# A low part of the weights on GpSimd once a block, and eight blocks a layer by seven products

## The chip, the cores and the metric

The kernel runs on one core of a Trainium2 chip. The metric is the device time of one execution in microseconds (us), as the median of several executions. Five engines work side by side, each through its own queue: TensorE (PE, with its weight loads as PEld), VectorE (DVE), ScalarE (ACT), GpSimd (POOL) and SyncE (SP).

## The reference

One decoder layer on 256 tokens of width 2048, all in float32: a gated feed-forward part, a token mixer, and a second feed-forward part, each with a residual and a layer norm. The change touches the two feed-forward parts alone.

```python
def swiglu(h, w_in, w_out):                       # w_in 2048 x 11264, w_out 5632 x 2048
    a, b = jnp.split(h @ w_in, 2, axis=-1)
    return (jax.nn.silu(a) * b) @ w_out

h = layer_norm(DN_ALPHA * h + 0.5 * swiglu(h, ffn1_w_in[l], ffn1_w_out[l]), ln1_g[l], ln1_b[l])
...                                               # attention, recurrent branch, merge, ln2
h = layer_norm(DN_ALPHA * h + 0.5 * swiglu(h, ffn2_w_in[l], ffn2_w_out[l]), ln3_g[l], ln3_b[l])
```

## The kernel before

**High and low parts.** TensorE multiplies in a rounded float format, so every operand is held as a high part (rounded) and a low part (the rest), and each product is three matmuls: high by high, high by low, low by high (`three`, lines 623 to 625). The activations are stationary and the weights stream. The weights come from HBM as float32 and are split on the way by `Weights.split_to`: ScalarE writes the high part `wh` (L217), VectorE subtracts it from the source and writes the low part `wl` (L218).

**Pieces.** The weights are one long list of pieces, in the order in which TensorE uses them. A plain piece is 128x1024 (two k-tiles by 512 columns); it is loaded into one of four `raw` buffers. The split runs four pieces ahead of TensorE (`AHEAD`), the load eight; `wh` and `wl` have five buffers each. `Weights.unit` hands TensorE the next slice and, at the start of each piece, sends off loads and splits.

**Blocks.** The input product of a feed-forward part is cut into 22 blocks of 512 columns (256 of each half). `blockF` runs one block over 16 k-tiles, as four chunks of four k-tiles. A chunk is done in one of two ways:

- plain (two pieces "c"): 4 k-tiles x 2 token tiles x 3 = 24 matmuls of 512 columns;
- by seven products in place of eight (Strassen's scheme; pieces `p1q3`, `p2`, `q5p7`, `q4p6` from one 128x2048 chunk `rf`, two buffers): 42 matmuls of 256 columns. Three sums of weight quarters are made on VectorE first (`Weights.operand`: `ws` of 1024 elements at L190, two of 512 at L194 and L197), and 3.5 pieces are split instead of two.

`block_plan` writes the order of a block's pieces. It also places pieces "o" there, the fills: plain pieces of the output product of an earlier segment, three at the start of a block from block 6 on and a fourth in the middle. When a fill has finished an output tile, ScalarE scales it (L960) and GpSimd issues a transfer that adds it to Y (L961). `FOUR` lists the blocks with all four chunks by seven products; from block 6 on, the others have chunk 0 plain. Blocks 0 and 1 are plain, block 2 has chunks 1 and 3 by seven products, blocks 3 to 5 have three. The last pieces of a part (`OUT_LAST`) are all plain.

**The join.** The seven products leave partial results in four PSUM banks. After a block, `gate` (inside `ffn`) joins them in the SBUF tile `z`, four quarters of 256: a copy on ScalarE (L920), then VectorE's joins, each with one input in PSUM (L921, L922, L923, L927 twice), then silu on ScalarE and the product on VectorE (L933). A block whose four chunks all go by seven products has a second L927 of 256 elements instead of 512.

**Who orders what.** The queues of TensorE, SyncE and GpSimd are in the order in which the code issues. Those of VectorE and ScalarE are ordered by a planner; `gate`'s first part is issued with high priority. Each engine runs its queue strictly in order.

Of the kernel before, what the change touches and what calls it, by code (L numbers as in the profile page):

```python
# [8 lines left out]
F32 = mybir.dt.float32  # L9
# [3 lines left out]
OP = mybir.AluOpType  # L13
AX = mybir.AxisListType.X

P = 128
# [5 lines left out]
NBK = NKF // 2  # L22
# [39 lines left out]
FORMS = ("p1q3", "p2", "q5p7", "q4p6")  # L62
# [6 lines left out]
def block_plan(chunks, fills, lead=2, n=4, late=True):  # L69

    plain = [("c", k) for q in range(n) if q not in chunks for k in (4 * q, 4 * q + 2)]
    forms = [(f, q) for q in chunks for f in FORMS]
    rest = ["o"] * fills
    plan = [(rest.pop(), 0) for _ in range(min(lead, fills))] + plain[:1]
    plain = plain[1:]
    slow = []
    while plain or rest:
        for which in (plain, rest) if late else (rest, plain):  # L80
            if which:
                p = which.pop(0)
                slow.append((p, 0) if p == "o" else p)
    if not forms:
        return plan + slow
    step = len(forms) / (len(slow) + 1)
    n = 0
    for i, f in enumerate(forms):
        plan.append(f)
        while len(slow) > n and i + 1 >= (n + 1) * step:  # L90
            plan.append(slow[n])
            n += 1
    return plan


FOUR = (9, 12, 15, 18, 21)


def layer_plans():
    three = (1, 2, 3)  # L100
    plans = [block_plan((), 0)] * 2
    plans += [block_plan((1, 3), 2, 0)] + [block_plan(three, 2, 2, late=False)] * 3
    for n in range(6, NBK):
        plans.append(block_plan(FAST if n in FOUR else three, 4, 3))
    return plans


FILLS = [(g, nb, 2 * p) for g, (b0, b1) in enumerate(SEGS[:-1]) for nb in range(4) for p in range(b1 - b0)]
PLANS = layer_plans()
PLAN_A = block_plan(FAST_A, 0, 0)  # L110
GATE_FAST = ((), (), (), (3,), FAST_A, FAST_A, (), ())
YA_FAST = ((), (0, 1), (0, 1), (0, 1))
# [4 lines left out]
MG_FORMS = (0, 1)  # L117
LAG_MG = (7, 4)
A_ORDER = (6, 7, None, 4, 5, 0, 1, 2, 3)
assert sum(f == "o" for p in PLANS for f, _ in p) == len(FILLS)  # L120

OUT_LAST = ([(nb, k) for nb in (0, 1) for k in (0, 2, 4)] + [(nb, 6) for nb in (0, 1)]
            + [(nb, k) for nb in (2, 3) for k in (0, 2, 4, 6)])
# [1 line left out]
LAG_T = (7, 6)  # L125
# [5 lines left out]
class Weights:  # L131
# [8 lines left out]
    def __init__(self, nc, pool, pieces, on_piece):  # L140
        self.nc, self.pool, self.on_piece = nc, pool, on_piece
        self.fast_pool = None
        self.pieces = pieces
        self.raw = {}
        self.sums = {}
        self.hl = {}
        self.loaded = 0
        self.split = 0
        self.cur = -1
        self.limit = None  # L150
        self.off = 0
# [50 lines left out]
    def split_to(self, i, step=PIECE):  # L202
        nc = self.nc
        while self.split <= min(i, len(self.pieces) - 1):
            form = self.pieces[self.split][1]
            self.load_to(self.split)
            k = self.key(self.split)
            h = self.pool.tile([P, PIECE], F32R, name=f"wh{self.split}", tag="wh", bufs=HL_BUFS)
            l = self.pool.tile([P, PIECE], F32R, name=f"wl{self.split}", tag="wl", bufs=HL_BUFS)
            n = self.size(self.split)  # L210
            if form:
                parts = [(self.operand(k, form), *(x[:, :n].rearrange("p (f r c) -> p f r c", r=2, c=256)
                                                   for x in (h, l)))]
            else:
                parts = [tuple(x[:, q:min(n, q + step)] for x in (self.raw[k], h, l)) for q in range(0, n, step)]
            for src, hp, lp in parts:
                nc.scalar.activation(hp, src, AF.Copy)  # L217
                self.last = nc.vector.tensor_tensor(lp, src, hp, op=OP.subtract)  # L218
            self.hl[self.split] = (h, l)
            if form in (None, FORMS[-1]):  # L220
                del self.raw[k]
            self.split += 1

    def unit(self, n):
        if self.cur < 0 or self.off == self.size(self.cur):
# [61 lines left out]
def tile_layer(ctx, tc, x_fm, x_tm, pos, f1a, f1o, wA, wki, wB, wG, lru, wab, wrb, wo, f2a, f2o,  # L287
               cols_d, ln1_g, ln1_b, ln2_g, ln2_b, ln3_g, ln3_b, out):
    nc = tc.nc
# [41 lines left out]
    def block_pieces(ap, plan, fills=None, fo=None):  # L331
        chunk = {}
        for f, k in plan:
            if f == "c":
                pieces.append((ap[:, k * 512:k * 512 + PIECE], None))
            elif f == "o":
                g, nb, k = next(fills)
                k += 2 * SEGS[g][0]
                pieces.append((fo[nb][:, k * 512:k * 512 + PIECE], None))
            else:  # L340
                if k not in chunk:
                    chunk[k] = ap[:, k * 2048:(k + 1) * 2048]
                pieces.append((chunk[k], f))

    def ffn_pieces(fa, fo):
        fills = iter(FILLS)
        for n, plan in enumerate(PLANS):
            block_pieces(fa[n], plan, fills, fo)
        for nb, k in OUT_LAST:
            k += 2 * SEGS[-1][0]  # L350
            plain([fo[nb][:, k * 512:k * 512 + PIECE]])

    ffn_pieces(f1a, f1o)
    for i, b in enumerate(A_ORDER):
        if b is None:
            plain([wki])
# [20 lines left out]
    for nb in range(3):  # L377
        block_pieces(wo[nb], block_plan(MG_FAST[nb], 0, 0))
    plain([wo[3]])
    ffn_pieces(f2a, f2o)  # L380

    W = Weights(nc, pool, pieces, bg.step)
    W.fast_pool = ctx.enter_context(tc.tile_pool(name="f1", bufs=1))
    lane, first_home, shared = [None], {}, ExitStack()

# [523 lines left out]
        if ln.last:  # L909
            ln.finish()  # L910

    def ffn(x, forms, ln):
        def gate(c, e, g, i, lag, plain):

            z = W.fast_pool.tile([P, 4 * S], F32, name=name("z"), tag="z", bufs=Z_BUFS)
            z4 = z.rearrange("p (j c) -> p j c", j=4)
            a, b = z4[:, 0:4:2], z4[:, 1:4:2]
            if e:
                p1, p6, p7, q5 = e[0][:, :S], e[0][:, S:], e[1][:, :S], e[1][:, S:]
                A.activation(z4[:, 0], p1, AF.Copy)  # L920
                V.tensor_tensor(z4[:, 1], z4[:, 0], p6, op=OP.add)  # L921
                V.tensor_tensor(z4[:, 2], z4[:, 1], p7, op=OP.add)  # L922
                V.tensor_tensor(b, q5[:, None, :].to_broadcast([P, 2, S]), z4[:, 1:3], op=OP.subtract)  # L923
                for t in range(2):
                    w = 512 if plain or t == 0 else S
                    zt = z[:, t * 512:t * 512 + w]
                    V.tensor_tensor(zt, zt, c[t][:, :w], op=OP.add)  # L927
                A.activation(a, a, AF.Silu)
            else:
                for t in range(2):  # L930
                    A.activation(z4[:, 2 * t], c[t][:, :S], AF.Silu)
                    A.activation(z4[:, 2 * t + 1], c[t][:, S:], AF.Copy)
            V.tensor_tensor(a, a, b, op=OP.mult)  # L933
            for _ in range(lag):
                yield
            ps = BP()
            for k in range(2):
                for t in range(2):
                    T.transpose(ps[:, k * S + t * P:k * S + (t + 1) * P], z[:, t * 512 + k * P:t * 512 + (k + 1) * P], ident)  # L939
            for k in range(2):  # L940
                hl = UHL("g")
                split(hl, ps[:, k * S:(k + 1) * S])
                g[i + k] = hl

        g = [[None] * (2 * (b1 - b0)) for b0, b1 in SEGS]
        fills = iter(FILLS)
        open_ps = []

        def fill():
            s, nb, k0 = next(fills)  # L950
            if k0 == 0:
                open_ps[:] = MM(), MM()
            for k in (k0, k0 + 1):
                w = W.unit(512)
                for t in range(2):
                    tokens(open_ps[t], g[s][k], t, w, k == 0, k == len(g[s]) - 1)
            if k0 + 2 == len(g[s]):
                for t in range(2):
                    u = W.fast_pool.tile([P, 512], F32, name=name("yd"), tag="yd", bufs=2)
                    A.activation(u, open_ps[t], AF.Copy, scale=0.5)  # L960
                    G.dma_start(Y[t][nb], u, accum_op=OP.add)  # L961

        for s, (b0, b1) in enumerate(SEGS):
            for n in range(b0, b1):
                c, e = blockF(x, forms, PLANS[n], fill)
                task = gate(c, e, g[s], 2 * (n - b0), LAG_T[n == NBK - 1], ("c", 0) in PLANS[n])
                with tc.high_priority():
                    next(task)
                bg.add("gate", task)
        new_stats()  # L970
        if not ln.last:
            share("t")
            bg.add("main", later(consts(), W.last.ins))
        out_product(g[-1], ln, pair=True)
# [7 lines left out]
                G.dma_start(away[t][nb], Y[t][nb])  # L982

    ln = InnerNorm("ln1_g", "ln1_b", FAST_A, put_away)
    ffn(xs, xf, ln)
    hs = ln.hs


# [346 lines left out]
    share("s")  # L1335


    ffn(ln.hs, ln.forms, OuterNorm(ln3_g, ln3_b))


def _layout(x, positions, ffn1_w_in, ffn1_w_out, ln1_g, ln1_b, w_in, conv_w, conv_b, lru_wa, lru_ba,
# [73 lines left out]
```

## Time and profile before

| | |
|---|---|
| median of 3 runs | 2387.85 us (2387.63 to 2387.97) |
| profiled execution | 2390.11 us, span 2388.3 us |
| TensorE busy | 2364.0 us, 99% |
| VectorE busy | 2213.3 us, 93% |
| ScalarE busy | 1502.0 us, 63% |
| GpSimd busy | 123.1 us, 5% |
| granted TensorE clock | 0.998 |

The span is the time from the first to the last instruction that the profiler saw; the execution's own time is a little longer. Matmul durations overlap in the records, so work on TensorE is read from starts. In the rows of the profile, L218 is line 218 of the kernel before, `out<-in` are the tiles, and what follows `<-` is what ended an idle time.

### The profile page before, as it was taken

The page shows a single profiled execution, that of the slowest core. Times are in us where ns is not written, and L with a number is a line of the kernel's source. Part 1 is how long each engine was busy: PE and PEld are TensorE (multiplying, and loading weights), DVE is VectorE, ACT ScalarE, POOL GpSimd, SP SyncE. Part 2 cuts the span into 40 slices and gives each one's busy share as a digit, 9 for nine tenths or more (in the row PEclk, how much of TensorE's full clock was granted, in tenths as well). Part 3 has the DMA queues.
Part 4 walks back from the last instruction along what each step waited for, and adds up shares of the span by engine and source line. Part 5 has one row for each costly group of instructions (what it writes and reads, how often), then busy time and mean ns, then how long its engine had stood idle before and what let it go on. Part 6 is the DMA issues. An engine that isn't in the chain of part 4 may idle for free.

```text
span 2388.3 us, 38774 instructions
## 1 busy us (share of the span) xinstructions
PE 2364.0 (99%) x14890; PEld 2111.6 (88%) x14890; DVE 2213.3 (93%) x3127; ACT 1502.0 (63%) x2042; POOL 123.1 (5%) x196
## 2 busy tenths in 40 slices
PE   8999999999999999999999999999999999999997
PEld 6898999989988888888999998888898899899996
DVE  7999999999999998789788888998999999999997
ACT  7666666666647554665588885555766666666662
POOL 0000000000000000001000001100000000000000
PEclk9999999999999999999999999999999999999999
DMA  8666666666666455547655568755675666666665
GB/s 293 193 222 213 227 212 217 219 217 212 195 210 221 177 186 179 187 142 265 207 183 185 187 191 295 252 194 175 209 229 212 221 212 188 230 227 212 216 208 176
DMA packets 123018, 501.24 MB, mean 210 GB/s; under 512 B 14256, under 2 KB 14256, under 8 KB 101968
## 3 DMA queue, kind: packets, MB, share of 16 engines
q1 hardware_dynamic: 104256, 454.60, 54.6%
q0 software_dynamic: 18576, 44.17, 8.1%
q8 instruction: 116, 1.90, 0.3%
q14 instruction: 70, 0.57, 0.1%
HBM read 467.26 MB, written 10.49 MB: 200 GB/s over the span
## 4 chain that ended last, share of the span: by engine, by line
PE 92%; DVE 5%; issue 1%; DMA 1%; ACT 0%; SPq 0%; POOL 0%; DVEq 0%; ACTq 0%; POOLq 0%
PE mm L625 20%; PE mm L623 20%; PE mm L624 20%; PE bp L624 6%; PE bp L623 6%; PE bp L625 6%; PE mm L1248 4%; PE mm L1249 4%; PE mm L1247 4%; DVE wl L218 2%; PE bp L939 1%; DVE ws L190 0%; ACT wh L217 0%; DMA raw<-f1a 0%; PE bp L1128 0%
## 5 line engine op out<-in xcount | busy, mean ns | idle before, releaser
L217 ACT ACTIVATE wh<-raw 128x1024 fp32r<-128x1024 f32 (+2 forms) x540 | 552.3, 1044 | 293.3 <-PE mm L625 169.0
L218 DVE TENSOR_TENSOR wl<-raw,wh 128x1024 fp32r<-128x1024 f32 (+2 forms) x540 | 637.2, 1196 | 96.4 <-ACT wh L217 94.7
L217 ACT ACTIVATE wh<-rf 128x1024 fp32r<-128x1024 f32 (+1 forms) x489 | 439.9, 915 | 313.6 <-PE mm L625 157.3
L218 DVE TENSOR_TENSOR wl<-rf,wh 128x1024 fp32r<-128x1024 f32 (+1 forms) x489 | 505.5, 1040 | 12.8 <-ACT wh L217 7.1
L623 PE MATMUL mm<-wh,hs 128*128 128x512 f32 (+1 forms) x884 | 317.0, 359 | 0.0
L625 PE MATMUL mm<-wh,hs 128*128 128x512 f32 (+1 forms) x884 | 311.1, 352 | 1.1 <-DVE hs L804 1.1
L624 PE MATMUL mm<-wl,hs 128*128 128x512 f32 (+1 forms) x884 | 310.8, 352 | 0.2 <-DVE wl L218 0.2
L625 PE MATMUL mm<-wh,g 128*128 128x512 f32 x704 | 278.2, 395 | 0.2 <-DVE g L747 0.2
L623 PE MATMUL mm<-wh,g 128*128 128x512 f32 x704 | 278.2, 395 | 0.0
L624 PE MATMUL mm<-wl,g 128*128 128x512 f32 x704 | 278.1, 395 | 0.0
L217 ACT ACTIVATE wh<-ws 128x1024 fp32r<-128x1024 f32 x163 | 173.0, 1061 | 141.9 <-PE mm L625 83.9
L623 PE MATMUL bp<-wh,sh 128*128 128x256 f32 x918 | 258.7, 282 | 0.0
L624 PE MATMUL bp<-wl,sh 128*128 128x256 f32 x918 | 256.4, 279 | 1.2 <-DVE wl L218 1.2
L625 PE MATMUL bp<-wh,sl 128*128 128x256 f32 x918 | 256.2, 279 | 0.0
L190 DVE TENSOR_TENSOR ws<-rf 128x1024 f32<-128x1024 f32 x163 | 198.4, 1217 | 7.0 <-DMA rf<-f1a 1.4
L218 DVE TENSOR_TENSOR wl<-ws,wh 128x1024 fp32r<-128x1024 f32 x163 | 198.2, 1216 | 2.8 <-ACT wh L217 2.4
L625 PEld LDWEIGHTS mm<-wh,hs 128*128 128x128 f32 x884 | 165.9, 188 | 27.5 <-DVE hs L804 2.5
L623 PEld LDWEIGHTS mm<-wh,hs 128*128 128x128 f32 x884 | 166.1, 188 | 24.3 <-issue 1.3
L624 PEld LDWEIGHTS mm<-wl,hs 128*128 128x128 f32 x884 | 166.1, 188 | 22.4 <-DVE wl L218 0.7
L1249 PE MATMUL mm<-hs,wl 128*128 128x256 f32 x640 | 179.8, 281 | 0.0
L1247 PE MATMUL mm<-hs,wh 128*128 128x256 f32 x640 | 179.8, 281 | 0.0
L1248 PE MATMUL mm<-hs,wh 128*128 128x256 f32 x640 | 179.8, 281 | 0.0
(312 smaller groups left out, 5291.8 us busy)
## 6 DMA issues: line engine op xcount, KB each, us to landing
rf<-f1a SPq DMA_DIRECT2D x64, 1024.0 KB, 5.4
rf<-f2a SPq DMA_DIRECT2D x64, 1024.0 KB, 5.6
raw<-f1o SPq DMA_DIRECT2D x88, 512.0 KB, 6.5
raw<-f2o SPq DMA_DIRECT2D x88, 512.0 KB, 6.6
raw<-wB SPq DMA_DIRECT2D x80, 512.0 KB, 4.1
raw<-wG SPq DMA_DIRECT2D x54, 512.0 KB, 4.3
raw<-f2a SPq DMA_DIRECT2D x48, 512.0 KB, 4.8
raw<-f1a SPq DMA_DIRECT2D x47, 512.0 KB, 5.3
```

What stands on the lines that cost most here:

```text
L190: v.tensor_tensor(t, b[:, 0:4:3], b[:, 1:2].to_broadcast([P, 2, 2, 256]), op=OP.add)
L217: nc.scalar.activation(hp, src, AF.Copy)
L218: self.last = nc.vector.tensor_tensor(lp, src, hp, op=OP.subtract)
L623: T.matmul(ps, xh, w[0], start=start, stop=False)
L624: T.matmul(ps, xh, w[1], start=False, stop=False)
L625: T.matmul(ps, xl, w[0], start=False, stop=stop)
L939: T.transpose(ps[:, k * S + t * P:k * S + (t + 1) * P], z[:, t * 512 + k * P:t * 512 + (k + 1) * P], ident)
L1247: T.matmul(ps[:, :S], w[0], x[:, 0], start=first, stop=False)
L1248: T.matmul(ps[:, :S], w[0], x[:, 1], start=False, stop=False)
L1249: T.matmul(ps[:, :S], w[1], x[:, 0], start=False, stop=last)
```

## The change

Three things. First, `FOUR` has eight blocks, every second one from 7 to 21, instead of five, and the first layer's block 2 has three chunks by seven products instead of two (`EARLY`, with a plan for each layer). Second, for each block that has a chunk by seven products, one plain piece two or three places into the next block is noted in `late`; `split_to` lets ScalarE make its high part as before, but puts the low part aside. Third, `gate` calls `late_parts` after the first join: GpSimd copies one element that this join wrote into a small tile, and then makes the low part that was put aside. That is 20 copies and 20 subtractions in each of the two feed-forward parts. The condition for the wide last join is now read from the plan's plain pieces in general.

```diff
-FOUR = (9, 12, 15, 18, 21)
-
-
-def layer_plans():
+FOUR = (7, 9, 11, 13, 15, 17, 19, 21)
+EARLY = (((), (), (1, 2, 3)), ((), (), (1, 3)))
+
+
+def layer_plans(early):
     three = (1, 2, 3)
-    plans = [block_plan((), 0)] * 2
-    plans += [block_plan((1, 3), 2, 0)] + [block_plan(three, 2, 2, late=False)] * 3
+    plans = [block_plan(early[n], 0) for n in range(2)]
+    plans += [block_plan(early[2], 2, 0)] + [block_plan(three, 2, 2, late=False)] * 3
     for n in range(6, NBK):
         plans.append(block_plan(FAST if n in FOUR else three, 4, 3))
     return plans
...
-PLANS = layer_plans()
+PLANS = [layer_plans(e) for e in EARLY]
...
                 nc.scalar.activation(hp, src, AF.Copy)
-                self.last = nc.vector.tensor_tensor(lp, src, hp, op=OP.subtract)
+                if self.split in self.late:
+                    self.waiting.append((lp, src, hp))
+                else:
+                    self.last = nc.vector.tensor_tensor(lp, src, hp, op=OP.subtract)
...
+    def late_parts(self, mark):
+
+        for lp, src, hp in self.waiting:
+            t = self.pool.tile([P, 32], F32, name=f"go{self.split}", tag="sm", bufs=20)
+            self.nc.gpsimd.tensor_copy(t[:, :1], mark)
+            self.nc.gpsimd.tensor_tensor(lp, src, hp, op=OP.subtract)
+        self.waiting = []
...
-    def ffn_pieces(fa, fo):
+    def ffn_pieces(fa, fo, plans):
         fills = iter(FILLS)
-        for n, plan in enumerate(PLANS):
+        ends = []
+        for n, plan in enumerate(plans):
             block_pieces(fa[n], plan, fills, fo)
+            if any(f in FORMS for f, _ in plan):
+                ends.append(len(pieces))
         for nb, k in OUT_LAST:
             k += 2 * SEGS[-1][0]
             plain([fo[nb][:, k * 512:k * 512 + PIECE]])
+        late.extend([i for i in (e + 3, e + 2) if not pieces[i][1]][0] for e in ends if not all(pieces[i][1] for i in (e + 2, e + 3)))
...
                 A.activation(z4[:, 0], p1, AF.Copy)
                 V.tensor_tensor(z4[:, 1], z4[:, 0], p6, op=OP.add)
+                W.late_parts(z4[:, 1, :1])
                 V.tensor_tensor(z4[:, 2], z4[:, 1], p7, op=OP.add)
                 V.tensor_tensor(b, q5[:, None, :].to_broadcast([P, 2, S]), z4[:, 1:3], op=OP.subtract)
...
-                task = gate(c, e, g[s], 2 * (n - b0), LAG_T[n == NBK - 1], ("c", 0) in PLANS[n])
+                task = gate(c, e, g[s], 2 * (n - b0), LAG_T[n == NBK - 1], any(f == "c" for f, _ in plans[n]))
```

More of the change, by code (lines that the diff above doesn't have):

```diff
@@ L119 @@
 A_ORDER = (6, 7, None, 4, 5, 0, 1, 2, 3)
-assert sum(f == "o" for p in PLANS for f, _ in p) == len(FILLS)
+assert sum(f == "o" for p in PLANS[0] for f, _ in p) == len(FILLS)
 OUT_LAST = ([(nb, k) for nb in (0, 1) for k in (0, 2, 4)] + [(nb, 6) for nb in (0, 1)]
@@ L142, in __init__ @@
         self.fast_pool = None
+        self.late = set()
+        self.waiting = []
         self.pieces = pieces
@@ L222, in split_to @@
             self.split += 1
+    def late_parts(self, mark):
[3 more added lines that the diff above has]
+            self.nc.gpsimd.tensor_tensor(lp, src, hp, op=OP.subtract)
+        self.waiting = []
     def unit(self, n):
@@ L351, in ffn_pieces @@
             plain([fo[nb][:, k * 512:k * 512 + PIECE]])
-    ffn_pieces(f1a, f1o)
+        late.extend([i for i in (e + 3, e + 2) if not pieces[i][1]][0] for e in ends if not all(pieces[i][1] for i in (e + 2, e + 3)))
+    late = []
+    ffn_pieces(f1a, f1o, PLANS[0])
     for i, b in enumerate(A_ORDER):
@@ L379, in tile_layer @@
     plain([wo[3]])
-    ffn_pieces(f2a, f2o)
+    ffn_pieces(f2a, f2o, PLANS[1])
     W = Weights(nc, pool, pieces, bg.step)
+    W.late.update(late)
     W.fast_pool = ctx.enter_context(tc.tile_pool(name="f1", bufs=1))
@@ L910, in out_product, with ffn @@
             ln.finish()
-    def ffn(x, forms, ln):
+    def ffn(x, forms, ln, plans):
         def gate(c, e, g, i, lag, plain):
@@ L964, in ffn @@
             for n in range(b0, b1):
-                c, e = blockF(x, forms, PLANS[n], fill)
-                task = gate(c, e, g[s], 2 * (n - b0), LAG_T[n == NBK - 1], ("c", 0) in PLANS[n])
+                c, e = blockF(x, forms, plans[n], fill)
+                task = gate(c, e, g[s], 2 * (n - b0), LAG_T[n == NBK - 1], any(f == "c" for f, _ in plans[n]))
                 with tc.high_priority():
@@ L984, in tile_layer @@
     ln = InnerNorm("ln1_g", "ln1_b", FAST_A, put_away)
-    ffn(xs, xf, ln)
+    ffn(xs, xf, ln, PLANS[0])
     hs = ln.hs
@@ L1335, in tile_layer @@
     share("s")
-    ffn(ln.hs, ln.forms, OuterNorm(ln3_g, ln3_b))
+    ffn(ln.hs, ln.forms, OuterNorm(ln3_g, ln3_b), PLANS[1])
 def _layout(x, positions, ffn1_w_in, ffn1_w_out, ln1_g, ln1_b, w_in, conv_w, conv_b, lru_wa, lru_ba,
```

## The prediction

> **What bounds the kernel now.** I read the page first: shares, the chain that ended last, and what TensorE waits for.
>
> ```profile
> span 2388.3 us, 38774 instructions
> ...
> PE 2364.0 (99%) x14890; PEld 2111.6 (88%) x14890; DVE 2213.3 (93%) x3127; ACT 1502.0 (63%) x2042; POOL 123.1 (5%) x196
> ...
> PE 92%; DVE 5%; issue 1%; DMA 1%; ACT 0%; SPq 0%; POOL 0%; DVEq 0%; ACTq 0%; POOLq 0%
> ...
> L624 PE MATMUL mm<-wl,hs 128*128 128x512 f32 (+1 forms) x884 | 310.8, 352 | 0.2 <-DVE wl L218 0.2
> ...
> L624 PE MATMUL bp<-wl,sh 128*128 128x256 f32 x918 | 256.4, 279 | 1.2 <-DVE wl L218 1.2
> ```
>
> TensorE is busy 99% of the span and 92% of the last chain. VectorE follows closely at 93%, yet TensorE's waits for the low parts that VectorE makes (L218) are only 1.2 + 0.2 = 1.4 us in all. So TensorE's count of columns sets the time, and VectorE just keeps up. How closely, I read from the busy time in three consecutive blocks in mid-layer, cut at the first join (L921) of each block: block 12 (all four chunks by seven products, "F"), then 13 and 14 (three chunks so and one plain, "T").
>
> ```profile
> core 0: us, PE busy (x) PEld busy (x) DVE busy (x) ACT busy (x) POOL busy (x), PEclk, DMA share, GB/s
> 355.13:386.40 31.27, 31.27 (x222) 29.07 (x221) 31.05 (x39) 20.92 (x26) 1.75 (x2) 1.00 0.70 213
> 386.40:418.10 31.70, 31.70 (x203) 28.46 (x202) 30.72 (x38) 20.29 (x25) 1.75 (x2) 1.00 0.65 221
> 418.10:450.29 32.19, 32.19 (x205) 28.84 (x204) 31.63 (x39) 19.71 (x25) 1.75 (x2) 1.00 0.62 214
> ```
>
> TensorE is busy for the whole of each at full granted clock (1.00). The three last 31.27 + 31.70 + 32.19 = 95.16 us, VectorE is busy for 31.05 + 30.72 + 31.63 = 93.40, so it is idle for 1.76 us in three blocks, 0.59 us a block. Any VectorE work beyond that becomes TensorE's wait.
>
> **TensorE's gain.** Durations of matmuls overlap, so I take starts, in the timeline of TensorE.
>
> ```profile
> 384.73 0.40 PE L623 MATMUL mm<-wh,g 128*128 128x512 f32 x1
> ...
> 387.52 0.40 PE L623 MATMUL mm<-wh,g 128*128 128x512 f32 x1
> ...
> 390.56 0.39 PE L624 MATMUL mm<-wl,g 128*128 128x512 f32 x1
> ...
> 395.93 0.28 PE L623 MATMUL bp<-wh,xs 128*128 128x256 f32 x1
> ...
> 445.81 0.28 PE L623 MATMUL bp<-wh,sh 128*128 128x256 f32 x1
> ...
> 448.61 0.40 PE L623 MATMUL mm<-wh,g 128*128 128x512 f32 x1
> ```
>
> From 387.52 to 395.93 stand three plain pieces, 36 matmuls of 512 columns: 8.41 / 36 = 0.2336 us each. From 445.81 to 448.61 stand 24 of 256 columns: 2.80 / 24 = 0.1167 us. A plain chunk is 24 of the former, 5.61 us; by seven products it is 42 of the latter, 4.90 us. A converted chunk gives 0.70 us. FOUR has eight blocks instead of five in each of two layers, and block 2 of the first layer gets a third chunk: 3 + 3 + 1 = 7 chunks, 7 x 0.705 = 4.9 us.
>
> **VectorE's price.** Starts again, at the end of block 12:
>
> ```profile
> 386.40 0.41 DVE L921 TENSOR_TENSOR z<-z,bp 128x256 f32<-128x256 f32 x1
> 386.73 1.22 DVE L218 TENSOR_TENSOR wl<-raw,wh 128x1024 fp32r<-128x1024 f32 x1
> 387.87 0.41 DVE L922 TENSOR_TENSOR z<-z,bp 128x256 f32<-128x256 f32 x1
> 388.20 1.22 DVE L190 TENSOR_TENSOR ws<-rf 128x1024 f32<-128x1024 f32 x1
> 389.33 0.68 DVE L923 TENSOR_TENSOR z<-bp,z 128x512 f32<-128x512 f32 x1
> 389.93 1.21 DVE L218 TENSOR_TENSOR wl<-rf,wh 128x1024 fp32r<-128x1024 f32 x1
> 391.07 1.01 DVE L927 TENSOR_TENSOR z<-z,mm 128x512 f32<-128x512 f32 x2
> 392.00 0.68 DVE L194 TENSOR_TENSOR rf<-ws,rf 128x512 f32<-128x512 f32 x1
> 392.60 0.68 DVE L218 TENSOR_TENSOR wl<-rf,wh 128x512 fp32r<-128x512 f32 x1
> ```
>
> Start to start, 1024 elements take 1.14 us, 512 take 0.60, a 256-wide join 0.33. A chunk by seven products needs three operand sums (1.14 + 0.60 + 0.60) and four low parts (3 x 1.14 + 0.60): 6.36. The plain chunk needs two low parts, 2.28, and a join that is 512 wide instead of 256, 0.27 more. So F costs VectorE 3.81 us more than T, and TensorE 0.70 less. From the three blocks: T is (93.40 - 3.81) / 3 = 29.86 for VectorE and (95.16 + 0.70) / 3 = 31.95 for TensorE, F is 33.67 and 31.25. With F and T in turn, a pair needs 63.5 us of VectorE and 63.2 of TensorE. Eight F blocks alone would overload VectorE by 0.3 us a pair.
>
> **What GpSimd takes off.** One low part a block, 1.14 us: 2 x 1.14 from a pair, which leaves VectorE 61.26 against 63.20. That is 0.97 us of spare a block, more than today's 0.59. Over the kernel 40 low parts leave VectorE (46 us) and 7 x 3.81 = 27 come. If the spare lasts, all of the 4.9 us arrive; where GpSimd's work costs VectorE over 0.97 us a block, it turns into TensorE's wait.
>
> **The added waits.** GpSimd copies one element of z after the first join, then subtracts. The copy waits for VectorE; behind it in GpSimd's queue are only the two transfers to Y of the next block's fill, due half a block later, and ScalarE's two buffers for those. The join into z's second and fourth quarters must now wait for that copy, since it overwrites what the copy reads, and all of VectorE's queue stands behind it. Rows for two such copies elsewhere in the kernel (VectorE's timeline, then GpSimd's) and, by groups, for GpSimd's DMA issues:
>
> ```profile
> 2356.33 1.21 DVE L218 TENSOR_TENSOR wl<-raw,wh 128x1024 fp32r<-128x1024 f32 x1
> ```
>
> ```profile
> 2356.48 1.10 POOL L856 COPY row<-st 128x1 f32<-128x1 f32 x1 [32.66 <-DVE st L757]
> ...
> 2358.98 0.22 POOL L856 COPY row<-st 128x1 f32<-128x1 f32 x1
> ```
>
> ```profile
> L961 POOL DMA_DIRECT2D y<-yd x80 | 70.1, 982 | 1212.5 <-ACT yd L960 1162.3 <-DVE rf L194 24.9 <-DVE wl L218 24.6
> L1200 POOL DMA_DIRECT2D gf<-gd x24 | 12.9, 540 | 11.1 <-DVE y L606 4.7 <-PE bp L1310 2.3 <-DVE y L608 1.2
> ```
>
> A copy alone takes 0.22 us. The one that started 0.15 us into a VectorE subtraction took 1.10 and ended at 2357.58, 0.04 after the subtraction did (2356.33 + 1.21). So a VectorE operation with both inputs in SBUF holds GpSimd off. In the changed program's instruction order one such operation (ws, 1.14, or rf, 0.60) and the second join stand between the first join and the join that waits; the copy can end while the second join runs, so I put this wait at nothing. If that cover were gone it would be up to 1.1 us a block, just over the spare.
>
> No row shows a 128x1024 subtraction on GpSimd. It is at least VectorE's 1.22 us, as I see no reason for it to be quicker. From above, its deadline bounds it. The late piece after a T block that an F block follows is the third fill: the next block began at 384.73, two pieces of 2.80 later its low part is read at 390.56, and the first join began at 386.40, so 4.16 us are left. After an F block the piece is the fourth, 2.80 later: 6.96 us. I take about 2.4 us, twice VectorE's: ends 3.5 to 4.0 us after the first join, inside both.
> The Trainium skill (GPSIMD Engine Reference, Performance versus the Vector engine) gives 4497 ns for an add of 2048 fp32 elements; half of it, my estimate from that page, is 2.25 us, and the sum stays as it is.
>
> Elsewhere: SyncE's queue is unaffected, since the raw buffer that frees some microseconds later is wanted four plain pieces on, most of a block. ScalarE gets seven times 1.5 pieces more and stands at 63%.
>
> **The sum.** Profiled execution 2390.11 us; less 4.9 for the columns; less 0.4 of the 1.4 us of waits for low parts (each early block gets 1.14 of relief, but the first layer's block 2 gets 3.81 of new work): 2384.8. The median of the runs lies 2.26 below the profiled execution (2387.85): **2382.5 us**.
>
> **Rival 1, slower: VectorE is held off in its turn.** The copy's row shows one direction. If GpSimd's subtraction, once begun, likewise holds off VectorE's operations with two SBUF inputs, only joins (one input in PSUM) can run beside it. In the changed order the joins aren't consecutive: after the first stand a two-input operation, the second join (0.33), a two-input low part, the third join (0.60), and then the last joins at once (T) or after another two-input sum (F). If GpSimd starts before that low part, VectorE loses 2.3 of the 2.4 us each time, 4.6 a pair: 61.26 + 4.6 = 65.9 against 63.4 now (two thirds of 95.16), 2.4 x 16 pairs = 39 us slower. If it starts one operation later, it has 1.80 us of joins beside it in T and 0.60 in F: the loss is 0.6 + 1.8, a pair 63.7, 0.2 x 16 = 4 us slower. It decides from 0.97 us a block. Range 2392 to 2427, middle 2409. For it: that one row. Against it: no VectorE operation in the rows above is drawn out, and the 80 transfers that L961 issues beside it are stretched themselves (0.98 against 0.54).
> The Trainium skill (SBUF — State Buffer, SBUF: two separate sides) speaks against this change: the port pair that both engines share is an exclusive lock for a whole instruction, in either direction. The copy agrees for one direction; by the page the time is this rival's.
>
> **Rival 2: the gain is eaten.** VectorE loses about what it was relieved of, 1 us a block; TensorE waits at the end of F blocks for part of what it gained: 2384 to 2392.
>
> **Rival 3, slower: GpSimd is late.** It waits through two or three VectorE operations and ends 5 us after the first join; the third fill waits 0.8 us at each of 8 x 2 such ends: 13 us, less the 4.9 gained: 2396. The deadline of 4.16 us is close; for F ends nothing happens.
>
> **How the numbers follow.** 0.2%, about what a measurement of this kernel can tell from no change, is 4.8 us: faster is below 2383.1. The forecast, with all of the spare left, has 0.56, between 2381 (all 1.4 us of waits gone too) and 2384.5; 0.45 of it below 2383.1. Rival 2 has 0.12, all within. Rival 1 has 0.24, 0.20 of it slower and 0.04 within; rival 3 has 0.08, slower. That makes 0.45, 0.27 and 0.28. The range goes from 2381 into rival 1, to 2402, beyond which lies some 0.17.
>
> **What would show it.** Right: block 12 and its like still without TensorE gaps, F and T in turn taking 63.2 us a pair, GpSimd's subtraction near 2.4 us, VectorE's spare near 1 us a block, its operations no longer than 1.22 us beside GpSimd. Rival 1: a two-input VectorE operation of 2 to 3.5 us, or a hole of that size, beside each subtraction, and TensorE waiting for L218's successor in F blocks. Rival 3: TensorE waiting for GpSimd at the third fill. A pair over 63.4 us makes the forecast wrong.

## The result: slower by 2.2%

| | before | after |
|---|---|---|
| median | 2387.77 us (2387.63 to 2387.97, 4 runs) | 2440.39 us (2439.81 to 2441.06, 4 runs) |
| profiled execution, span | 2390.11, 2388.3 | 2439.81, 2438.0 |

The ratio is 1.0218, 95% interval 1.0206 to 1.0231: 52.6 us slower. The forecast was 2382.5, the range ended at 2402. The mechanism is the prediction's Rival 1, in its strong case.

The page of the changed kernel: the span, the busy times, the shares of the chain that ended last, and three groups of TensorE's matmuls with their idle time and what ended it.

```profile
span 2438.0 us, 39174 instructions
...
PE 2378.7 (98%) x15016; PEld 2118.5 (87%) x15016; DVE 2279.0 (93%) x3122; ACT 1500.4 (62%) x2056; POOL 248.5 (10%) x276
...
PE 56%; DVE 28%; issue 11%; ACT 4%; DMA 1%; ACTq 0%; DVEq 0%; POOL 0%; SPq 0%; POOLq 0%
...
L643 PE MATMUL mm<-wh,hs 128*128 128x512 f32 (+1 forms) x872 | 312.1, 358 | 5.4 <-DVE z L948 5.4
...
L644 PE MATMUL mm<-wl,g 128*128 128x512 f32 x704 | 280.4, 398 | 15.8 <-DVE wl L224 15.8
...
L644 PE MATMUL bp<-wl,sh 128*128 128x256 f32 x924 | 261.1, 283 | 9.8 <-DVE wl L224 9.8
```

VectorE has five instructions fewer than before and is busy for 66 us more. Its share of the last chain went from 5% to 28%, and TensorE's waits for low parts (L218 before, L224 now) from 1.4 us to 25.8 (15.8 and 9.8 in these rows, 0.2 in a group that isn't shown). TensorE never waits for GpSimd.

The same stretch as in the prediction, cut at the first join (now L941), for an F block's window and a T block's:

```profile
463.04:496.64 33.60, 31.98 (x221) 29.20 (x220) 33.31 (x38) 20.46 (x26) 4.70 (x4) 1.00 0.68 210
496.64:529.10 32.46, 32.28 (x205) 28.62 (x203) 32.28 (x37) 19.70 (x25) 5.24 (x4) 1.00 0.59 205
sum 66.06, PE 64.26 PEld 57.82 DVE 65.60 ACT 40.16 POOL 9.94; mean PE 32.13 PEld 28.91 DVE 32.80 ACT 20.08 POOL 4.97
```

A pair takes 66.06 us; two thirds of the three blocks before were 63.44. The cause is in VectorE's timeline at the end of a T block, beside GpSimd's, and in one row from the end of an F block:

```profile
463.04 0.42 DVE L941 TENSOR_TENSOR z<-z,bp 128x256 f32<-128x256 f32 x1
463.37 0.69 DVE L200 TENSOR_TENSOR rf<-rf 128x512 f32<-128x512 f32 x1
463.97 0.42 DVE L943 TENSOR_TENSOR z<-z,bp 128x256 f32<-128x256 f32 x1
464.30 2.70 DVE L224 TENSOR_TENSOR wl<-rf,wh 128x512 fp32r<-128x512 f32 x1
466.93 0.68 DVE L944 TENSOR_TENSOR z<-bp,z 128x512 f32<-128x512 f32 x1
...
498.44 3.23 DVE L224 TENSOR_TENSOR wl<-rf,wh 128x1024 fp32r<-128x1024 f32 x1
```

```profile
463.52 0.58 POOL L234 COPY go<-z 128x1 f32<-128x1 f32 x1 [4.38 <-DVE z L941]
464.06 2.39 POOL L235 TENSOR_TENSOR wl<-raw,wh 128x1024 fp32r<-128x1024 f32 x1
...
498.20 2.39 POOL L235 TENSOR_TENSOR wl<-raw,wh 128x1024 fp32r<-128x1024 f32 x1
```

GpSimd's subtraction runs from 464.06 to 466.45. The join L943, which has one input in PSUM, ends beside it as always. The next operation has both inputs in SBUF and takes 2.70 us instead of 0.68: it ends at 467.00, 0.55 after GpSimd has let go. At the end of the F block a low part of 1024 takes 3.23 instead of 1.22. This happens at 38 of the 40 subtractions; the last one of each part stands beside other work. So a subtraction holds VectorE for 2.0 us and has taken 1.14 off it: some 77 us of hold over the kernel, against 46 us of relief.

### The profile page after: what moved, and what is told of

It reads as the page before. It is cut to its first block, busy times and chain, and to the rows that moved or that the text cites. A ratio compares the mean times of both kernels' runs of the same rounds, so it can differ in the third digit from the quotient of the medians.

```text
span 2438.0 us, 39174 instructions
## 1 busy us (share of the span) xinstructions
PE 2378.7 (98%) x15016; PEld 2118.5 (87%) x15016; DVE 2279.0 (93%) x3122; ACT 1500.4 (62%) x2056; POOL 248.5 (10%) x276
## 4 chain that ended last, share of the span: by engine, by line
PE 56%; DVE 28%; issue 11%; ACT 4%; DMA 1%; ACTq 0%; DVEq 0%; POOL 0%; SPq 0%; POOLq 0%
DVE wl L224 14%; PE mm L644 12%; PE mm L645 12%; PE mm L643 12%; DVE ws L193 4%; PE mm L1269 4%; PE mm L1268 4%; PE mm L1270 4%; ACT wh L220 4%; PE bp L644 2%; PE bp L643 2%; PE bp L645 2%; DVE rf L200 2%; DVE rf L197 2%; DVE z L948 2%
## 5 line engine op out<-in xcount | busy, mean ns | idle before, releaser
L220 ACT ACTIVATE wh<-raw 128x1024 fp32r<-128x1024 f32 (+3 forms) x526 | 537.0, 1043 | 250.7 <-PE mm L645 131.2
L224 DVE TENSOR_TENSOR wl<-raw,wh 128x1024 fp32r<-128x1024 f32 (+3 forms) x486 | 574.4, 1195 | 84.9 <-ACT wh L220 83.1
L220 ACT ACTIVATE wh<-rf 128x1024 fp32r<-128x1024 f32 (+1 forms) x510 | 455.5, 913 | 303.2 <-DVE rf L200 179.6
L224 DVE TENSOR_TENSOR wl<-rf,wh 128x1024 fp32r<-128x1024 f32 (+1 forms) x510 | 602.9, 1191 | 11.5 <-ACT wh L220 5.5
L643 PE MATMUL mm<-wh,hs 128*128 128x512 f32 (+1 forms) x872 | 312.1, 358 | 5.4 <-DVE z L948 5.4
L645 PE MATMUL mm<-wh,hs 128*128 128x512 f32 (+1 forms) x872 | 305.0, 350 | 1.1 <-DVE hs L824 1.1
L644 PE MATMUL mm<-wl,hs 128*128 128x512 f32 (+1 forms) x872 | 304.7, 349 | 0.2 <-DVE wl L224 0.2
L644 PE MATMUL mm<-wl,g 128*128 128x512 f32 x704 | 280.4, 398 | 15.8 <-DVE wl L224 15.8
L220 ACT ACTIVATE wh<-ws 128x1024 fp32r<-128x1024 f32 x170 | 180.1, 1059 | 146.9 <-PE mm L645 81.6
L193 DVE TENSOR_TENSOR ws<-rf 128x1024 f32<-128x1024 f32 x170 | 207.2, 1219 | 4.6 <-DMA rf<-wG 1.1
L224 DVE TENSOR_TENSOR wl<-ws,wh 128x1024 fp32r<-128x1024 f32 x170 | 207.0, 1218 | 2.3 <-ACT wh L220 2.3
L644 PEld LDWEIGHTS bp<-wl,sh 128*128 128x128 f32 x924 | 173.7, 188 | 17.0 <-DVE wl L224 13.4
```

Of the source, the lines that this page charges most:

```text
L193: v.tensor_tensor(t, b[:, 0:4:3], b[:, 1:2].to_broadcast([P, 2, 2, 256]), op=OP.add)
L643: T.matmul(ps, xh, w[0], start=start, stop=False)
L644: T.matmul(ps, xh, w[1], start=False, stop=False)
L645: T.matmul(ps, xl, w[0], start=False, stop=stop)
```

## Experiments

Each is the changed kernel with the edit shown. Ratios are to runs of the kernel before on the same chip (medians 2387.97 to 2388.23).

### Which part is it?

**Nothing on GpSimd** (`e1`), with all eight F blocks:

```diff
-    W.late.update(late)
```

> The changed kernel's eight F blocks and its third early chunk, but every low part stays on VectorE: nothing is put on GpSimd. Theory (each GpSimd subtraction holds off a VectorE operation with two SBUF inputs): without the 40 subtractions the two-input operations are back at 0.68 and 1.22 us, a pair F + T takes 63.5 us, VectorE's need, and the run lies near the kernel before, 2384 to 2394. Rival A (eight F blocks overload VectorE, and the lock is a side show): a pair stays near 66 us and the run near 2430 or above, since VectorE gets back the 46 us of low parts as well. Rival B (the early chunk is to blame): layer 1's early blocks keep most of their loss, about 10 us over the kernel before.

Measured 2396.01 us, ratio 1.0033 (1.0021 to 1.0045). It is 2 us above the range that I gave. Of the 52.6 us, 44 go with GpSimd's work. Eight F blocks without relief cost 8 us; the pair's windows say why:

```profile
482.45:513.59 31.14, 31.14 (x201) 27.97 (x200) 30.77 (x38) 19.54 (x25) 1.75 (x2) 1.00 0.59 206
513.59:546.40 32.81, 32.51 (x225) 29.91 (x224) 32.70 (x41) 21.04 (x27) 1.75 (x2) 1.00 0.69 221
sum 63.95, PE 63.65 PEld 57.88 DVE 63.47 ACT 40.58 POOL 3.50; mean PE 31.82 PEld 28.94 DVE 31.74 ACT 20.29 POOL 1.75
```

VectorE is busy for 63.47 us of a pair (the prediction's sum had 63.5) and the pair takes 63.95. Rivals A and B fall: no pair near 66, and no loss of 10 us in the early blocks.

**The copies alone** (`e3`):

```diff
-                else:
-                    self.last = nc.vector.tensor_tensor(lp, src, hp, op=OP.subtract)
+                self.last = nc.vector.tensor_tensor(lp, src, hp, op=OP.subtract)
...
-            self.nc.gpsimd.tensor_tensor(lp, src, hp, op=OP.subtract)
```

> The changed plans; GpSimd's copy of one element after the first join is kept, and with it the wait of the third join; the subtraction itself stays on VectorE in its usual place. Theory: a copy of one element holds nothing for long, so the same as the run with nothing on GpSimd, within 3 us. Rival C (the third join waits for the copy, which itself is held off by a two-input operation): up to 1.1 us x 40 more than that run, 20 to 40 us.

Measured 2396.05 us, the same as with nothing on GpSimd. The copies are held off (1.09 us on average), but the third join's wait for them costs nothing.

**The plans of before, with GpSimd's low parts** (`e2`):

```diff
-FOUR = (7, 9, 11, 13, 15, 17, 19, 21)
-EARLY = (((), (), (1, 2, 3)), ((), (), (1, 3)))
+FOUR = (9, 12, 15, 18, 21)
+EARLY = (((), (), (1, 3)), ((), (), (1, 3)))
```

> The plans of the kernel before (five F blocks a layer, two early chunks), and GpSimd makes the 40 late low parts. Theory: each costs VectorE 2.0 us of being held and saves it 1.14, 0.9 us a block more against a spare of 0.59, so 0.3 us x 32 blocks, and some 4 us for each layer's early blocks: slower, 2400 to 2412. Rival A (the F blocks are the cause): VectorE is relieved by 1.14 a block and TensorE has nothing new: 2386 to 2388.

Measured 2439.83 us, 1.0214 (1.0197 to 1.0231). So GpSimd's work alone costs what the whole change costs, and Rival A falls for good. But my figure was too low by 28 us. Part of the rest is in another group of VectorE, the first sum of a chunk (here L193), which waits for the transfer of its weights; the same group of the kernel before (L190) stands below it.

```profile
L193 DVE TENSOR_TENSOR ws<-rf 128x1024 f32<-128x1024 f32 x163 | 198.7, 1219 | 29.0 <-DMA rf<-f1a 12.6 <-DMA rf<-f2a 10.9 <-DMA rf<-wab 1.7
```

```profile
L190 DVE TENSOR_TENSOR ws<-rf 128x1024 f32<-128x1024 f32 x163 | 198.4, 1217 | 7.0 <-DMA rf<-f1a 1.4 <-DMA rf<-wab 1.4 <-DMA rf<-wG 1.2
```

VectorE idles for 22 us more there. Why the transfers come late with these plans wasn't tried, and stays open.

### What does GpSimd hold, and when?

**Fill instead of subtract** (`e6`). The order on VectorE is that of the changed kernel.

```diff
-            self.nc.gpsimd.tensor_tensor(lp, src, hp, op=OP.subtract)
+            self.nc.gpsimd.memset(lp.bitcast(F32), 0.0)
```

> As the changed kernel, with its order on VectorE, but GpSimd fills the low part with zeros (memset) instead of subtracting: that low part is left out of the product, and GpSimd reads nothing from SBUF. Theory in its narrow form (the held-off engine waits while the other reads two SBUF inputs): the two-input operation beside the memset stays at 0.68 or 1.22 us, VectorE keeps the 1.14 us a block, and the run is at 2382 to 2386, what the offload would be worth without the hold. Wide form (any GpSimd instruction on SBUF takes the port for its length): the operation is drawn out by the memset's length, which no row shows; if that is about 1 us, VectorE breaks even and the run lies at 2392 to 2400. Rival (GpSimd's instruction count or its semaphores are what costs): about 2440.

Measured 2383.13 us, 0.9980 (0.9971 to 0.9989): faster than before. VectorE's timeline, GpSimd's, and the sum of a pair's windows:

```profile
508.74 0.41 DVE L943 TENSOR_TENSOR z<-z,bp 128x256 f32<-128x256 f32 x1
509.07 0.68 DVE L224 TENSOR_TENSOR wl<-rf,wh 128x512 fp32r<-128x512 f32 x1
509.67 0.68 DVE L944 TENSOR_TENSOR z<-bp,z 128x512 f32<-128x512 f32 x1
```

```profile
508.80 0.95 POOL L235 MEMSET wl<- 128x1024 f32 x1
```

```profile
sum 63.21, PE 63.21 PEld 57.72 DVE 61.77 ACT 40.96 POOL 6.96; mean PE 31.61 PEld 28.86 DVE 30.88 ACT 20.48 POOL 3.48
```

The same two-input operation runs wholly beside the memset and takes its usual 0.68. The pair takes 63.21, TensorE's own need in the prediction (63.2).

**Copy instead of subtract** (`e10`): `tensor_copy(lp, src)` in that place.

> As the changed kernel, with its order on VectorE, but GpSimd copies the raw piece into the low part instead of subtracting: the values of that low part are not the product's, and GpSimd reads one SBUF input instead of two (the memset read none and held nothing). If two inputs on both sides are needed for the hold: as the memset, 2382 to 2386, and the two-input operation beside it stays at 0.68 or 1.22 us. If one input on GpSimd's side is enough: that operation is drawn out by about the copy's length, which I put at 1 to 2.4 us, and the run lies between 2396 and 2440.

Measured 2388.00 us, 0.9999 (0.9990 to 1.0009). VectorE, then GpSimd:

```profile
511.56 1.32 DVE L224 TENSOR_TENSOR wl<-rf,wh 128x512 fp32r<-128x512 f32 x1
```

```profile
511.30 1.04 POOL L235 CAST wl<-raw 128x1024 fp32r<-128x1024 f32 x1
```

One input on GpSimd's side is enough: 0.68 becomes 1.32. The copy was quicker than I had put it (1.04 us), so the run came out below the 2396 that I gave for this case: what is held, 0.64, is less than the 1.14 saved.

**Half the columns** (`e7`):

```diff
-                    self.waiting.append((lp, src, hp))
+                    self.last = nc.vector.tensor_tensor(lp[:, 512:], src[:, 512:], hp[:, 512:], op=OP.subtract)
+                    self.waiting.append((lp[:, :512], src[:, :512], hp[:, :512]))
```

> As the changed kernel, but GpSimd subtracts columns 0 to 511 of the late piece and VectorE the other 512. Theory: the subtraction takes 1.2 us; where a two-input operation meets it, VectorE is held for 0.8 to 1.2 us and has saved 0.54, so the loss a block is 0.3 to 0.6 us, half or a third of the changed kernel's 0.9: 2400 to 2420, between nothing on GpSimd (2396) and all of it (2440). Rival (the hold is a fixed price of starting an instruction on GpSimd, whatever its length): held 2 us as before and less saved, 2440 to 2465.

Measured 2413.80 us, 1.0108 (1.0092 to 1.0123). In the two timelines:

```profile
521.00 1.58 DVE L200 TENSOR_TENSOR rf<-rf 128x512 f32<-128x512 f32 x1
```

```profile
520.75 1.28 POOL L236 TENSOR_TENSOR wl<-raw,wh 128x512 fp32r<-128x512 f32 x1
```

1.28 us of GpSimd hold 0.90 (1.58 instead of 0.68). The hold goes with the length of GpSimd's instruction; it is no fixed price.

These three and the result agree with the Trainium skill (SBUF — State Buffer, Who interferes with whom): by it a VectorE instruction with two SBUF inputs contends with a GpSimd instruction that reads SBUF, and not with one that only writes it.

### Can the hold be covered?

**Joins one behind the other** (`e5`). The sums and low parts that stood between VectorE's joins are queued behind the last join; GpSimd's part is unchanged.

```diff
+    def queue(self, ins):                    # around each sum and low part of a weight piece
+        if self.behind:
+            self.tc.add_manual_dep(ins.ins, self.behind, ...)       # issue order alone
+        return ins
...
-                    V.tensor_tensor(zt, zt, c[t][:, :w], op=OP.add)
+                    end = V.tensor_tensor(zt, zt, c[t][:, :w], op=OP.add)
+                W.behind = end.ins.name
```

> As the changed kernel, but VectorE's five joins of a block are queued one behind the other, and the sums and low parts that stood between them come behind the last. Theory: the subtraction (2.39 us) starts some 0.65 us after the first join and the joins last 2.46 us (T) or 2.19 (F), so a two-input operation is held 0.6 to 0.9 us instead of 2.0; VectorE keeps 0.2 to 0.5 us a block of the 1.14 saved, a pair takes 63.2 to 63.5: 2383 to 2392. Rival A (F blocks) and rival C (third join's wait, which is kept): no better than the changed kernel, about 2440. Rival D (GpSimd slows joins from PSUM too): the joins are drawn out and the run stays above 2410.

Measured 2386.60 us, 0.9994 (0.9984 to 1.0003), 54 us less than the changed kernel with the same work on the same engines. VectorE, GpSimd, and the pair's sum:

```profile
508.94 0.41 DVE L949 TENSOR_TENSOR z<-z,bp 128x256 f32<-128x256 f32 x1
509.39 0.42 DVE L951 TENSOR_TENSOR z<-z,bp 128x256 f32<-128x256 f32 x1
509.91 0.69 DVE L952 TENSOR_TENSOR z<-bp,z 128x512 f32<-128x512 f32 x1
510.64 1.29 DVE L956 TENSOR_TENSOR z<-z,mm 128x512 f32<-128x512 f32 x2
511.84 0.69 DVE L198 TENSOR_TENSOR rf<-ws,rf 128x512 f32<-128x512 f32 x1
```

```profile
509.42 0.18 POOL L241 COPY go<-z 128x1 f32<-128x1 f32 x1 [4.24 <-DVE z L949]
509.56 2.42 POOL L242 TENSOR_TENSOR wl<-raw,wh 128x1024 fp32r<-128x1024 f32 x1
```

```profile
sum 63.45, PE 63.45 PEld 57.78 DVE 62.12 ACT 41.03 POOL 8.61; mean PE 31.73 PEld 28.89 DVE 31.06 ACT 20.52 POOL 4.30
```

The subtraction lies beside the joins from 509.56 to 511.98; they last as long as alone, and the sum behind them takes its 0.69. The copy, beside a join, takes 0.18 instead of 0.58 to 1.1. At the end of an F block, where the last join is shorter, the sum behind the joins takes 1.47 us instead of 1.22, so 0.25 of the hold is left there. That is less than I expected, but a pair still takes 0.25 us more than 63.20: TensorE waits some 0.2 us late in the F block.

**The same order, nothing on GpSimd** (`e8`: `e5` without the line that `e1` removes).

> VectorE's joins one behind the other, as in the run that did best, and nothing on GpSimd. If that run's gain over the changed kernel comes from GpSimd working beside the joins, VectorE is short of the 1.14 us a block again: 2394 to 2400, as the run with nothing on GpSimd in the old order (2396). If the new order alone is what helped, 2386 to 2388.

Measured 2404.72 us, 1.0070 (1.0053 to 1.0086). The order by itself loses 8.7 us against `e1`, where I expected it to change little; with GpSimd beside the joins it is 18 us better than without. So what helps is GpSimd's work under the cover of the joins, not the order by itself.

**Each subtraction twice** (`e11`: `e5` with the subtraction's line written a second time).

> Joins one behind the other with GpSimd beside them, but GpSimd does each subtraction twice (the second gives the same result). The first is covered by the joins, the second by nothing. Theory: each second subtraction holds a two-input operation for 2.2 to 2.4 us, VectorE needs 4.4 to 4.8 us more a pair, 60.75 + 4.6 + 1 of idle = 66.3 against 63.46: 2425 to 2440. Rival (what the new order brought was room on VectorE's queue, not cover): GpSimd's second instruction costs nothing until its due time, 2387 to 2395.

Measured 2467.46 us, 1.0334 (1.0318 to 1.0349), beyond what I gave. The second subtraction, which nothing covers, holds a two-input operation as before (one of 512 took 2.82 us). What I left out is that GpSimd itself then comes late; TensorE's largest wait:

```profile
PE mm L653 <- POOL wl L243: 45.7, 22, 2.3
```

**The plans of before, joins together** (`e12`: `e5` with the plans of `e2`).

> The plans of the kernel before (five F blocks, two early chunks), joins one behind the other, GpSimd's low parts beside them. VectorE is relieved and TensorE's columns are those of the kernel before: 2386 to 2388, if the seven converted chunks had brought little in the run with eight F blocks; from the columns alone it should be up to 4.9 us behind that run, 2386.6 + 4.9 = 2391.5 at most.

Measured 2389.46 us, 1.0006 (0.9997 to 1.0015): 2.9 us behind `e5`. Of the 4.9 us of the seven converted chunks, about 2.9 arrive with four pieces ahead; the intervals of the two ratios overlap, so the size is uncertain.

### How much of the columns' gain is there?

**11 F blocks** (`e9`: `e5` with F, F, T from block 6).

> Joins one behind the other with GpSimd beside them, and 11 F blocks a layer instead of eight (two F, one T). VectorE: 2 F + T = 93.0 us against TensorE's 94.5 by the sums of the prediction, so it would still fit on average, and three more F a layer give 6 x 0.70 = 4.2 us: 2382 to 2384. Against it: in the run with eight, TensorE already waits some 0.2 us in each F block, and two F in a row leave VectorE 1 us further behind before a T block lets it catch up: 2388 to 2396.

Measured 2404.95 us, 1.0070 (1.0055 to 1.0085). This is above both cases. The sum in the expectation is too low: the prediction's own figures give 2 x (33.67 - 1.14) + (29.86 - 1.14) = 93.8 us for VectorE, not 93.0. The windows of `e18`, the same blocks with more lead, show below what VectorE really needs.

**Five pieces ahead** (`e13`: `e5` with more lead).

```diff
-U_BUFS = 53
+U_BUFS = 49
...
-HL_BUFS = 5
-AHEAD = 4
+HL_BUFS = 6
+AHEAD = 5
```

> The best version so far (joins one behind the other, GpSimd beside them, eight F blocks), with the weights split five pieces ahead instead of four (six high and low buffers, four fewer of the shared ones). TensorE's last 0.26 us a pair there are low parts that are late at the end of an F block, while VectorE idles 1.7 us in the T block before, having reached the end of its lead. If the lead is what bounds it, a pair goes to 63.2: 2382 to 2384. If the sums (one buffer) or ScalarE bound how far ahead VectorE can go: no change, 2386 to 2388; if the transfers come late with one more piece held: 2390 to 2400.

Measured 2381.10 us, 0.9970 (0.9959 to 0.9982). This beats both kernels, by 6.9 and 59 us, and is just below the 2382 that I gave. A pair takes 63.21 us. Whether the lead did it, three runs with the same constants tell.

The kernel before with them (`e14`: the edits of `e1` and `e2`, and the constants):

> The kernel before, with its weights split five pieces ahead instead of four (six high and low buffers, four fewer of the shared ones); nothing on GpSimd. If the gain of the best version is the lead's: 2381 to 2383. If it is the offload's: TensorE had only 1.4 us of waits for low parts to lose, so 2386 to 2389.

Measured 2388.21 us, 1.0000 (0.9990 to 1.0009): the lead alone brings nothing.

Eight F blocks, nothing on GpSimd (`e15`):

> The changed plans with nothing on GpSimd (2396.0 with four pieces ahead), now with five. If VectorE's work bounds it on average (62.99 us of a pair's 63.95 busy), a longer lead saves only the idle 0.8 us a pair at most: 2386 to 2396. If the lead alone is what the best version gained from: 2381 to 2384.

Measured 2390.10 us, 1.0010 (1.0001 to 1.0020): 5.9 us better than `e1`, and still no gain on the kernel before. VectorE's busy time in a pair of `e1` is 63.47, as shown there, not 62.99, so the lead had 0.5 us of idle time to save; a pair now takes 63.60.

The changed kernel with them, in its own order (`e17`):

> The changed kernel as it is (its own order on VectorE, GpSimd's subtractions held against two-input operations), with five pieces ahead. VectorE's loss of 2 us a subtraction is work it lacks on average, so a lead cannot hide it: 2425 to 2440. If the hold is only a matter of timing, that a longer lead absorbs: below 2400.

Measured 2429.94 us, 1.0173 (1.0156 to 1.0190). The lead takes 10 us off and leaves the rest: the hold takes time that VectorE lacks on average, and is not only a matter of timing.

11 F blocks with them (`e16`):

> The best version (joins one behind the other, GpSimd beside them, five pieces ahead) with 11 F blocks a layer. By the sums VectorE needs 93.0 us against TensorE's 94.5 in F, F, T, and the columns give up to 4.2 us more: 2377 to 2380. With four pieces ahead the same 11 blocks cost 18 us (2405), because two F in a row put VectorE behind; if one more piece does not bridge that, 2383 to 2400.

Measured 2426.33 us, 1.0161 (1.0146 to 1.0176), worse than any case I gave. VectorE's timeline shows that this run tested something else:

```profile
427.22 1.22 DVE L194 TENSOR_TENSOR ws<-rf 128x1024 f32<-128x1024 f32 x1
428.36 0.41 DVE L951 TENSOR_TENSOR z<-z,bp 128x256 f32<-128x256 f32 x1
428.69 3.23 DVE L225 TENSOR_TENSOR wl<-rf,wh 128x1024 fp32r<-128x1024 f32 x1
```

With more lead, sums that were issued ahead of a block's end came between the joins again, and the hold was back (3.23 instead of 1.22; at 22 of the 40 subtractions it is 2.0 us). So these were queued behind the last join too (`W.recent` holds those of the newest piece), with 11 F blocks (`e18`) and with eight (`e19`):

```diff
                 W.behind = end.ins.name
+                for o in W.recent:
+                    tc.add_manual_dep(o, W.behind, ...)
```

> 11 F blocks a layer, five pieces ahead, GpSimd beside the joins, and now also the sums and low parts traced ahead of a block's end stand behind its last join (in 10 of 40 blocks one low part is left between the first join and the second, ahead of GpSimd's start). By the sums VectorE fits (93.0 of 94.5 us in F, F, T): 2377 to 2381 if the lead bridges two F in a row; 2384 to 2400 if it does not; over 2400 only if the subtractions are held against two-input operations still.

Measured 2399.56 us, 1.0051 (1.0036 to 1.0067): 27 us better, and the long holds are gone, but still slower than the kernel before. The sum of the windows of one T and two F blocks:

```profile
sum 96.33, PE 95.33 PEld 86.99 DVE 95.11 ACT 60.53 POOL 13.89; mean PE 31.78 PEld 29.00 DVE 31.70 ACT 20.18 POOL 4.63
```

VectorE is busy for 95.11 us, more than the 94.5 that TensorE needs. So with 11 F blocks VectorE doesn't fit even on average, and my 93.0 was wrong; `e9` and `e18` can't tell whether the lead would bridge two F blocks in a row if it did.

> The best version (eight F blocks, five pieces ahead, GpSimd beside the joins) with nothing at all left between the joins. TensorE had no wait for low parts left in a pair (63.21 us, its own need), so nothing is to be gained there: 2380 to 2382.

Measured 2380.67 us, 0.9969 (0.9956 to 0.9981), level with `e13` within the noise. In its pair's windows TensorE is busy throughout, and its need is that of the prediction:

```profile
476.56:507.41 30.85, 30.85 (x199) 27.80 (x198) 30.24 (x36) 19.43 (x26) 4.36 (x4) 1.00 0.60 217
507.41:539.76 32.35, 32.35 (x227) 29.92 (x226) 31.98 (x38) 20.54 (x26) 4.30 (x4) 1.00 0.72 216
sum 63.20, PE 63.20 PEld 57.72 DVE 62.22 ACT 39.98 POOL 8.67; mean PE 31.60 PEld 28.86 DVE 31.11 ACT 19.99 POOL 4.33
```

## Why the prediction was wrong

**The step that failed** is "if the spare lasts, all of the 4.9 us arrive", taken over Rival 1: the sum has no term for what GpSimd's subtraction costs VectorE. The runs showed 2.0 us at 38 of 40 subtractions, against a spare of 0.97 us a block. The prediction had a row for the hold in one direction (a copy of 1.10 us) and argued against the other that no VectorE operation in its rows was drawn out. But GpSimd's only reads of SBUF in those rows were of one element. The rows could not speak against it; I read silence as evidence and gave the rival 0.24. Experiments `e6`, `e7` and `e10` show the hold by what it depends on: that GpSimd reads, and for how long.

**What the prediction cited and set aside.** What the Trainium skill says of the shared port pair (SBUF — State Buffer, SBUF: two separate sides) is what the trace shows: VectorE is held in its turn, for what is left of GpSimd's instruction (2.0 of 2.39 us).

**Rival 1's number was near for mid-layer, its range too short.** It gave 65.9 us a pair, 66.06 was measured, and the change in order that decides (GpSimd starts ahead of the two-input low part) is the one that occurred at both ends. That the two figures lie so close is partly luck: the hold was 2.0 us and not 2.3, which alone makes the rival's pair 65.3, and VectorE is busy for 65.60 and idle for 0.46, which the rival didn't have. By the timelines of the first join, the changed kernel falls behind by 19.6 us from block 6 to block 21 of the first part (198.75 against 195.36, then 694.84 against 671.86) and by 19.7 in the second: 39.3 over 15 pairs, where the rival's sum had 39 over 16. The rest lies ahead of block 6 (3.4 in the first part, net of a first join that came 3.0 earlier than before, and 4.3 in the second) and around the end of the first part (3.2), where GpSimd makes low parts too: 50.2 in all, with 49.7 between the two profiled executions. The rival counted the 16 pairs alone, and so its own range ended at 2427.

**TensorE's gain was right.** A pair without waits takes 63.2 us, as `e6` (63.21) and `e19` (63.20) show. With the hold gone the forecast 2382.5 stands beside 2383.1 measured (`e6`). VectorE's spare there is 0.7 us a block (63.21 less 61.77 in a pair), less than the 0.97 forecast.

**VectorE's price was right as a sum, wrong as a limit.** Without GpSimd a pair keeps VectorE busy for 63.47 us (63.5 forecast), but "overload by 0.3 us a pair" came out as 63.95 against 63.20, 0.75: VectorE's need explains 0.27 of it, and in the other 0.48 it is idle. By the sums an F block needs more of VectorE than TensorE's time for it, and with four pieces ahead VectorE can't work far enough in advance; `e13` (63.45 to 63.21 a pair) and `e15` (63.95 to 63.60) show the lead's part. So the whole change, with the hold covered (`e5`), brought 1.4 us, within the noise, and not 5.3, until the lead was longer as well (`e19`: 7.6).

**The added waits.** The subtraction was put at 2.4 us and took 2.39. The third join's wait was put at nothing, and `e3` shows nothing. Rival 3's deadline was met with room (the subtraction ends 3.4 us after the first join at a T end, 4.0 at an F end, of 4.16 and 6.96); it decides when GpSimd's work is doubled (`e11`, 45.7 us of waits). Rival 2 was not what happened: at break-even it needed a loss of 1 us a block, and 2.0 was measured.

## What to carry to other kernels

In these runs, work that reads SBUF, moved from VectorE to GpSimd, was free only beside VectorE's joins, which take one of their inputs from PSUM: count what VectorE does in that time, by operand, and put such operations there in one stretch. Where a trace holds no instance of an interaction, its silence is no evidence against it. Spare time averaged over blocks is worth only as much as the lead lets the engine work ahead (`e5` against `e13`), and whether there is any is read from the windows of a run, not from a sum alone (`e18`).

## What the runs showed of the hardware

The hold was expected as a possibility; its limits were not. A memset of 128x1024 on GpSimd (0.95 us) held nothing, a copy with one SBUF input (1.04 us) held a two-input VectorE operation for 0.64 us, subtractions of 1.28 and 2.39 us for 0.90 and 2.0. Joins with one input in PSUM ran beside a subtraction of 2.42 us at their usual 0.41 to 0.42 and 0.69. A held VectorE operation of 512 elements ended 0.55 us after GpSimd's, one of 1024 1.08 us after, each some 0.13 less than its own length (0.68 and 1.22).
